# Two branches' gates as seven half-size products: the memory branch's gates and half of the banded one's in a hybrid decoder layer

## The chip, the cores and the metric

The kernel runs on one core of a Trainium2 chip. The metric is device time in microseconds (us) for one execution of the whole layer, from inputs in HBM to the output in HBM; the figure is the median of three runs. A profile of one further execution gives start and length of every instruction. The engines are called as the profile calls them: PE (matrix products; its weight loads are PEld), DVE and ACT (elementwise work), POOL (elementwise work and transfers it issues), SP (issues transfers).

## What is computed

One decoder layer for 512 tokens of width 1024, in float32. Three attention branches work on the normed input `u` (banded attention with sinks, number 0; stick-breaking attention, 1; attention to a memory of 256 entries, 2). Each branch's output goes through a projection of its own and is multiplied by a gate, a sigmoid of a product of `u` with a 1024 x 1024 weight. The sum goes through `w_out`, a norm and a residual, and then a SwiGLU feed-forward part (FFN) of width 2816.

```python
u = rms_norm(h, ln_mix_pre[l])
proj = jnp.einsum('bsd,de->bse', u, w_in[l])
qa, ka, va, qb, kb, vb, qm, gl = jnp.split(proj, split_idx, axis=-1)
...
g = jax.nn.sigmoid(gl.reshape(B, S, N_BRANCH, D))
merged = (g[:, :, 0] * jnp.einsum('bse,ed->bsd', y_swa, w_branch_swa[l])
          + g[:, :, 1] * jnp.einsum('bse,ed->bsd', y_sb, w_branch_sb[l])
          + g[:, :, 2] * jnp.einsum('bse,ed->bsd', y_mem, w_branch_mem[l]))
mix = jnp.einsum('bsd,de->bse', merged, w_out[l])
```

## The kernel before

Every float32 operand of a product is split in two parts, `hi` (rounded, ACT, line 134) and `lo` (the rest, DVE, line 135). A product is three matmuls, hi with hi, lo with hi, hi with lo (`mm3`, lines 166, 168, 169). Activations lie transposed: eight tiles `u[k]` of 128 features x 512 tokens, each as hi and lo (`n0h`, `n0l` to `n7h`, `n7l` in the profile).

The products with weights form one stream, `dn`, a `Stream` of units. A unit is 512 KB of weights (128 x 1024): it is loaded by SP up to four units ahead (`w_load`, three buffers `raw`), split up to three units ahead (`w_split`, four buffers each `hi` and `lo`), and multiplied by a generator of matmuls. Attention is written as generators too; between their steps `dn.run(us)` lets about so many microseconds of the stream through, so that PE has weights to multiply while ACT and DVE work on a softmax. `dn.until(flag)` runs the stream to a mark. A scheduler then orders each engine's instructions by priority, which is the order of writing except where `tc.high_priority()` lifts something, and by what it believes ready.

A gate unit (`proj` with kind `g0`, `g1` or `g2`) gives 128 gate features: 8 slices of K times 3 matmuls of 128 x 512 into one PSUM bank from `dps`, a pool of two banks, then one copy or sigmoid by ACT (lines 301 and 185). Each branch has eight gate units, and then four units of its projection (`branch`, tile `br`), whose results DVE multiplies with the gates (line 444). The order is: stick-breaking gates, four query units `qm`, stick-breaking projection; banded gates `g00` to `g07`, with the banded attention's last step and the scores of the first memory pair (`ms`) around them; banded projection, with the softmax (`mnm`, `mw`) and transposes (`mpt`) of the memory pairs; memory gates `g20` to `g27`; memory projection; `w_out` (`mx`).

The FFN's gate and up products are already made of seven half-size products each (`gu`, tiles `gx`, `gy`, `gw`; 128 x 256 matmuls), in the order p1 p5 p6 p3 p7 p2 p4, with banks from a larger pool, and nine `raw` buffers. There three sums of weights are made by transfers that add into `raw` (POOL queue, line 1015) or by DVE (line 1033); snapshots are copied by ACT (line 1053) and joined by DVE (line 1059).

Of the kernel before, what the change touches and what calls it, by code (L numbers as in the profile page):

```python
# [10 lines left out]
F32 = mybir.dt.float32  # L11
# [6 lines left out]
P = 128  # L18
# [14 lines left out]
class Stream:  # L33
# [12 lines left out]
    def add(self, src, n, mm):  # L46
        self.units.append({"src": src, "n": n, "mm": mm, "load": [], "split": [], "flags": []})
# [56 lines left out]
def tile_kernel(ctx, tc, a):  # L104
# [24 lines left out]

    st = {}  # L130

    def split(raw, hi, lo):

        ins = nc.scalar.copy(hi, raw)  # L134
        lows = nc.vector.tensor_tensor(lo, raw, hi.bitcast(F32), op=ALU.subtract)  # L135
        if "behind" in st:
            after(ins, st["behind"][0])
            after(lows, st["behind"][1])
        return ins
# [2 lines left out]

    def w_load(src, n):
        uid[0] += 1
        raw = wp.tile([P, 1024], F32, tag="raw", name=f"raw{uid[0]}")
        nc.sync.dma_start(raw[:, :n], src)
        return raw

    def w_split(raw, n):
        uid[0] += 1  # L150
        hi = wp.tile([P, 1024], F32R, tag="hi", name=f"hi{uid[0]}", bufs=4)
        lo = wp.tile([P, 1024], F32R, tag="lo", name=f"lo{uid[0]}", bufs=4)
        if isinstance(raw, list):
            for i, x in enumerate(raw):
                ins = split(x[:, :], hi[:, i * 512 : (i + 1) * 512], lo[:, i * 512 : (i + 1) * 512])
        else:
            ins = split(raw[:, :n], hi[:, :n], lo[:, :n])
        if "chain" in st:
            after(ins, st["chain"])
        return hi, lo  # L160
# [22 lines left out]
    def fn(*args, **kw):  # L183

        ins = nc.scalar.activation(*args, **kw)  # L185
        for p in pin:
            after(ins, p)
        since.append(ins)
        return ins
# [140 lines left out]
    def sigmoids(b):  # L330

        st.setdefault("sigmoid", set()).add(b)
        for c in range(8):
            if (f"g{b}", c) in st:
                g = st[(f"g{b}", c)]
                fn(g[:, :], g[:, :], AF.Sigmoid)

    def val(h, q):
        def gen(hi, lo):
# [94 lines left out]
    def branch(b, c2, order):  # L434
        def gen(hi, lo):
            for i in range(2):
                c = 2 * c2 + i
                g = st[(f"g{b}", c)]
                ps = dps(f"br{b}{c}")
                for k in range(4):  # L440
                    mm3(ps[:, :], cols((hi, lo), (i * 4 + k) * P, P), y[(b, k)], k == 0, k == 3)
# [26 lines left out]
    def add_proj(kind, idx, ci):  # L468
        src = a["w_p"][:, ci].rearrange("p k n -> p (k n)")
        dn.add(src, 1024, gate(int(kind[1]), idx) if kind[0] == "g" else proj(kind, idx))  # L470
# [10 lines left out]
    add_proj("qa", 2, 14)  # L481
    add_proj("qa", 3, 15)
    for b, order in ((SB, 0), (SWA, 1), (MEM, 2)):
        for c in range(8):
            add_proj(f"g{b}", c, 17 + 3 * c + b)
        dn.mark(f"gates{b}")
        if b == SB:
            for i in range(4):
                add_proj("qm", i, 8 + i)
        for c2 in range(4):  # L490
            dn.add(a["w_br"][:, b, 2 * c2 : 2 * c2 + 2].rearrange("p c k n -> p (c k n)"), 1024, branch(b, c2, order))
        dn.mark(f"branch{b}")
# [15 lines left out]

    FIRST = 3
    PIECE = ((0, 2), (2, 5), (5, 8))  # L510
    raws = [wp.tile([P, 1024], F32, tag="raw", name=f"raw_first{i}") for i in range(FIRST)]
    his = [wp.tile([P, 1024], F32R, tag="hi", name=f"hi_first{i}", bufs=4) for i in range(FIRST)]
    los = [wp.tile([P, 1024], F32R, tag="lo", name=f"lo_first{i}", bufs=4) for i in range(FIRST)]

# [323 lines left out]
    for c in range(4):  # L838
        for us in swa_pair(c, bias):
            dn.run(us)  # L840
    dn.until(f"gates{SWA}")
    table("sigmoid_and_others")
    sigmoids(SWA)
# [540 lines left out]
def _layout(i):  # L1384
# [10 lines left out]
    heads = np.concatenate([np.r_[c * 64 : c * 64 + 64, 256 + c * 64 : 256 + c * 64 + 64] for c in range(4)])  # L1395
    cols += [heads[c * P : (c + 1) * P] for c in range(4)]
    cols += [np.arange(512, 640)]
    cols += [np.arange(2816 + b * D + c * P, 2816 + b * D + (c + 1) * P) for c in range(8) for b in range(3)]
    w_mem = i["w_mem_kv"][0]
    br = [i["w_branch_swa"][0][heads], i["w_branch_sb"][0], i["w_branch_mem"][0]]  # L1400
    br = np.stack([kpn(w, P) for w in br])
# [46 lines left out]
```

## Time and profile before

| | us |
|---|---|
| median of three runs (811.13 to 811.83) | 811.28 |
| the profiled execution, device time | 811.55 |
| the profiled execution, span of the instructions | 809.4 |

The span and the device time of the same execution differ by 2.15 us, which lie around the instructions. In the profile "busy" is the time in which an engine had an instruction in it; matmuls overlap, so the distance between starts, and not the length of one, tells how fast PE works. The stages by span: projections and stick-breaking attention to 218 us, banded attention with the stick-breaking projection to 281, banded gates to 329, banded projection and memory attention to 365, memory gates to 408, memory projection and `w_out` to 460, then FFN up to about 700 and FFN down to the end.

### The profile page before, as it was taken

Reading aid. Unit: us, or ns where it says so; the run is one execution under the profiler, and the core shown is the slowest. Engines: PE = TensorE matmul, PEld = TensorE weight load, DVE = VectorE, ACT = ScalarE, POOL = GpSimd, SP = SyncE. Lnnn points to the kernel's source line nnn. Section 1 sums busy time; section 2 is a strip of 40 time slices with the busy share of each in tenths; the row PEclk is TensorE's granted clock in tenths of the full one; section 3 lists DMA queues with packets and bytes.
Section 4 is the critical chain, followed back from the end, with each engine's and each line's share of the span. In section 5 each row is a group of like instructions: output and inputs, shape, how many; then the busy total and the mean of one; then the engine's idle time right before and its main releaser. Section 6 shows DMA issues by size and latency. Waiting matters only on the chain.

```text
span 809.4 us, 12343 instructions
## 1 busy us (share of the span) xinstructions
PE 800.0 (99%) x4723; PEld 702.6 (87%) x4723; DVE 575.3 (71%) x917; ACT 458.8 (57%) x824; POOL 84.4 (10%) x103
## 2 busy tenths in 40 slices
PE   9999999999999999999999999999999999999996
PEld 6899788778788888888888899999999999988885
DVE  5898678646378832772284869977676777898797
ACT  6566677666756544552362566654444454666573
POOL 1001210000000000221004100010000000205200
PEclk9999999999999999999999999999999999999999
DMA  8343354211221233213259936987777662759902
GB/s 270 118 143 105 114 186 141 93 53 53 79 79 53 79 88 95 79 53 104 82 162 386 251 56 143 265 217 197 187 181 191 177 170 86 177 132 220 213 0 104
DMA packets 37739, 112.93 MB, mean 140 GB/s; under 512 B 4624, under 2 KB 6176, under 8 KB 37680
## 3 DMA queue, kind: packets, MB, share of 16 engines
q1 hardware_dynamic: 29232, 86.20, 33.5%
q0 software_dynamic: 8016, 25.68, 16.6%
q8 instruction: 37, 0.61, 0.3%
q10 hardware_dynamic: 432, 0.27, 0.1%
q14 instruction: 22, 0.18, 0.1%
HBM read 108.46 MB, written 3.67 MB: 139 GB/s over the span
## 4 chain that ended last, share of the span: by engine, by line
PE 93%; DVE 4%; ACT 2%; issue 1%; DVEq 0%; ACTq 0%
PE g L166 5%; PE g L168 5%; PE g L169 5%; PE gx L169 5%; PE gx L166 5%; PE gx L168 5%; PE z L172 4%; PE br L168 3%; PE br L166 3%; PE br L169 3%; PE x L166 2%; PE x L169 2%; PE x L168 2%; PE gy L169 2%; PE gy L166 2%; PE gy L168 2%
## 5 line engine op out<-in xcount | busy, mean ns | idle before, releaser
L135 DVE TENSOR_TENSOR lo<-raw,hi 128x1024 fp32r<-128x1024 f32 (+2 forms) x64 | 78.8, 1236 | 74.1 <-ACT hi L134 74.1
L134 ACT CAST hi<-gw 128x1024 fp32r<-128x1024 f32 x77 | 79.8, 1047 | 81.4 <-DVE gw L1033 39.8
L134 ACT CAST hi<-raw 128x1024 fp32r<-128x1024 f32 (+2 forms) x64 | 65.7, 1034 | 95.2 <-PE g L168 61.7
L135 DVE TENSOR_TENSOR lo<-gw,hi 128x1024 fp32r<-128x1024 f32 x77 | 93.6, 1224 | 34.0 <-ACT hi L134 33.9
L1015 POOL DMA_DIRECT2D gw<-in_w_gu x27 | 23.4, 896 | 188.2 <-DMA gw<-in_w_gu 81.9
L134 ACT CAST hi<-r 128x1024 fp32r<-128x1024 f32 (+1 forms) x24 | 23.6, 981 | 19.9 <-PE y L169 5.3
L168 PE MATMUL x<-lo,lh 128*128 128x512 f32 x88 | 34.3, 389 | 0.0
L166 PE MATMUL x<-hi,lh 128*128 128x512 f32 x88 | 34.3, 389 | 0.0
L169 PE MATMUL x<-hi,ll 128*128 128x512 f32 x88 | 34.1, 389 | 0.0
L135 DVE TENSOR_TENSOR lo<-r,hi 128x1024 fp32r<-128x1024 f32 (+1 forms) x24 | 27.2, 1135 | 3.7 <-ACT hi L134 3.6
L185 ACT ACTIVATE e<-e 128x384 f32<-128x384 f32 (+1 forms) x48 | 26.9, 561 | 1.5
L679 DVE SCALAR_TENSOR_TENSOR e<-z,e 128x384 f32<-128x384 f32 (+1 forms) x24 | 14.4, 598 | 17.6 <-ACT e L185 17.6
L135 DVE TENSOR_TENSOR lo<-bp,hi 128x512 fp32r<-128x512 f32 x33 | 22.8, 727 | 5.7 <-ACT hi L134 5.6
L134 ACT CAST hi<-bp 128x512 fp32r<-128x512 f32 x33 | 19.2, 620 | 13.3 <-PE y L169 4.8
L169 PE MATMUL gx<-N2h,lo 128*128 128x256 f32 x88 | 25.0, 284 | 0.3 <-DVE lo L135 0.3
L166 PE MATMUL gx<-B11h,hi 128*128 128x256 f32 x88 | 25.1, 285 | 0.2 <-ACT B11h L944 0.2
L166 PE MATMUL mx<-woh,mgh 128*128 128x512 f32 x64 | 25.0, 391 | 0.0
L169 PE MATMUL gw<-B21h,lo 128*128 128x256 f32 x88 | 25.0, 284 | 0.0
L168 PE MATMUL gx<-B11l,hi 128*128 128x256 f32 x88 | 25.0, 284 | 0.0
L169 PE MATMUL mx<-woh,mgl 128*128 128x512 f32 x64 | 24.9, 390 | 0.0
L169 PE MATMUL gy<-T1h,lo 128*128 128x256 f32 x88 | 24.9, 283 | 0.0
L168 PE MATMUL gw<-B21l,hi 128*128 128x256 f32 x88 | 24.9, 283 | 0.0
(764 smaller groups left out, 2797.8 us busy)
## 6 DMA issues: line engine op xcount, KB each, us to landing
gw<-in_w_gu SPq DMA_DIRECT2D x57, 512.0 KB, 5.1
raw<-in_w_p SPq DMA_DIRECT2D x38, 512.0 KB, 3.6
gw<-in_w_gu POOLq DMA_DIRECT2D x27, 512.0 KB, 7.1
raw<-in_w_br SPq DMA_DIRECT2D x12, 512.0 KB, 3.6
bp<-in_w_dn SPq DMA_DIRECT2D x22, 256.0 KB, 8.2
r<-in_w_dn POOLq DMA_DIRECT2D x10, 512.0 KB, 8.3
raw<-in_w_out SPq DMA_DIRECT2D x8, 512.0 KB, 3.6
bp<-in_w_dn POOLq DMA_DIRECT2D x11, 256.0 KB, 12.8
```

What stands on the lines that cost most here:

```text
L134: ins = nc.scalar.copy(hi, raw)
L135: lows = nc.vector.tensor_tensor(lo, raw, hi.bitcast(F32), op=ALU.subtract)
L166: one = nc.tensor.matmul(out, lh, rh, start=start, stop=False, skip_group_check=True)
L168: nc.tensor.matmul(out, *two, start=False, stop=False, skip_group_check=True)
L169: return one, nc.tensor.matmul(out, *three, start=False, stop=stop, skip_group_check=True)
L172: return nc.tensor.matmul(out, l, r, start=start, stop=stop, skip_group_check=True)
L185: ins = nc.scalar.activation(*args, **kw)
L679: nc.vector.scalar_tensor_tensor(x, z[i][:, :n], 0.0, x, op0=ALU.max, op1=ALU.add)
L1015: nc.gpsimd.dma_start(gw[(n, key)][:, :], g_src(n, i, j), accum_op=ALU.add)
```

## The change

For the memory branch, the eight gate units become two groups (`n` = 0, 1) of seven units; of the banded branch, gate units 0, 1, 4, 5 stay, and 2, 3, 6, 7 become one such group (`n` = 1). A group covers four gate tiles: weights are cut in two halves of gate tiles (`f`) by two halves of K (`j`), tokens in two halves of 256. Each unit is still 512 KB of weights, or a sum of such, and 24 matmuls, now of 128 x 256.

- Left sides: p1, p2, p4 use quarters of the weight as loaded. `s` starts as the sum of two quarters (a load, and a POOL transfer that adds) for p5; DVE adds p1's quarter for p6 and then p2's for p3 (`q_sum`), and p3 takes it with the sign turned. `t` is another sum by load and adding transfer, for p7.
- Right sides: p1, p2, p3 use halves of `u` as they are. `rights` builds the sides of p6, p7 and p4 from `u` once (tiles `fx`, `fy`, `ft`, `fp6`, `fp7`, `fp4`, split to `p6r`, `p7r`, `p4r`), after the last banded pair. `right_t1` writes the split of `ft` over the second half of `u[0]` to `u[3]`, for p5, once the last plain gate unit is through.
- Results: bank `x` takes p1, p6, p7 and p4 on top of each other, `y` p5 and p3, `w` p2. ACT copies the bank after p1, p5 and p6 (`qk`); DVE joins after p2, p3 and p7. The three tiles come from the same pool of two banks. Sigmoids are of 128 x 256, eight for a group.
- `raw` has five buffers in place of three. On the host the gate columns of `w_p` stand branch by branch.

```diff
-    def split(raw, hi, lo):
-
-        ins = nc.scalar.copy(hi, raw)
-        lows = nc.vector.tensor_tensor(lo, raw, hi.bitcast(F32), op=ALU.subtract)
+    def split(raw, hi, lo, sign=1.0):
+
+        if sign == 1.0:
+            ins = nc.scalar.copy(hi, raw)
+            lows = nc.vector.tensor_tensor(lo, raw, hi.bitcast(F32), op=ALU.subtract)
+        else:
+            ins = nc.scalar.mul(hi, raw, sign)
+            lows = nc.vector.scalar_tensor_tensor(lo, raw, sign, hi.bitcast(F32), op0=ALU.mult, op1=ALU.subtract)
...
-        raw = wp.tile([P, 1024], F32, tag="raw", name=f"raw{uid[0]}")
+        raw = wp.tile([P, 1024], F32, tag="raw", name=f"raw{uid[0]}", bufs=5)
...
+        for args in st.pop(("raw", b), ()):
+            gate_out(b, *args)
+
+    def gate_out(b, n, i, f, src, sign=1.0):
+
+        for j in range(2):
+            c = 4 * f + 2 * n + j
+            if (b, c) not in quart:
+                quart[(b, c)] = ck(f"g{b}{c}")
+            g = quart[(b, c)]
+            fn(g[:, i * 256 : (i + 1) * 256], src[:, j * 256 : (j + 1) * 256], AF.Sigmoid, scale=sign)
+
+    quart = {}
+    right = {}
+    TILE = dict(p1="x", p6="x", p7="x", p4="x", p5="y", p3="y", p2="w")
+    SEVEN = ("p1", "p2", "p5", "p6", "p3", "p7", "p4")
+    qw, qb_, qk = {}, {}, {}
+
+    def right_of(p, k):
+        if p in ("p1", "p2"):
+            return tuple(x[:, :256] for x in u[k if p == "p1" else 4 + k])
+        if p in ("p5", "p3"):
+            return tuple(x[:, 256:] for x in u[k if p == "p5" else 4 + k])
+        return cols(right[p][k // 2], (k % 2) * 256, 256)
+
+    def q_src(b, n, f, j):
+        c = 17 + 8 * b + 4 * f + 2 * n
+        return a["w_p"][:, c : c + 2, 4 * j : 4 * j + 4].rearrange("p g k n -> p g (k n)")
+
+    def q_raw(b, n, key, f, j):
+        uid[0] += 1
+        raw = wp.tile([P, 1024], F32, tag="raw", name=f"qw{uid[0]}", bufs=5)
+        nc.sync.dma_start(raw[:, :].rearrange("p (g m) -> p g m", g=2), q_src(b, n, f, j))
+        qw[(b, n, key)] = raw
+
+    def q_plus(b, n, key, f, j):
+        raw = qw[(b, n, key)]
+        nc.gpsimd.dma_start(raw[:, :].rearrange("p (g m) -> p g m", g=2), q_src(b, n, f, j), accum_op=ALU.add)
+
+    def q_got(b, n, p):
+        key = {"p5": "s", "p6": "s", "p3": "s", "p7": "t"}.get(p, p)
+
+        def got():
+            if (b, n, key) not in qw:
+                q_raw(b, n, key, *{"p1": (0, 0), "p2": (0, 1), "p4": (1, 1)}[p])
+            raw = qw[(b, n, key)]
+            return (raw, -1.0) if p == "p3" else raw
+
+        return got
+
+    def q_sum(b, n, key):
+        def add():
+            x, y = qw[(b, n, "s")], qw[(b, n, key)]
+            nc.vector.tensor_tensor(x[:, :], x[:, :], y[:, :], op=ALU.add)
+
+        return add
+
+    def q_end(b, n, p, ps):
+        def done(i, f, src, sign=1.0):
+            if b in st.get("sigmoid", ()):
+                gate_out(b, n, i, f, src, sign)
+                return
+            if sign != 1.0:
+                t = ck(f"qr{b}{n}")
+                nc.scalar.mul(t[:, :], src[:, :], sign)
+                src = t
+            st.setdefault(("raw", b), []).append((n, i, f, src))
+
+        def join(t, x, y, op, i, f):
+            nc.vector.tensor_tensor(t[:, :], x[:, :], y[:, :], op=op)
+            done(i, f, t)
+
+        with tc.high_priority():
+            if p in ("p1", "p5", "p6"):
+                qk[p] = ck(f"qk{p}{b}{n}")
+                nc.scalar.copy(qk[p][:, :], ps[:, :])
+            elif p == "p3":
+                t = qk.pop("p6")
+                join(t, t, ps, ALU.subtract, 1, 0)
+            elif p == "p7":
+                t = qk.pop("p5")
+                join(t, t, ps, ALU.subtract, 1, 1)
+            elif p == "p2":
+                t = ck(f"qj{b}{n}")
+                join(t, ps, qk.pop("p1"), ALU.add, 0, 0)
+            else:
+                done(0, 1, ps, -1.0)
+
+    def quarter(b, n, p):
+        def gen(hi, lo):
+            if p in ("p1", "p5", "p2"):
+                qb_[TILE[p]] = dps(f"q{TILE[p]}{b}{n}")
+            ps = qb_[TILE[p]]
+            for j in range(2):
+                for k in range(4):
+                    first = p in ("p1", "p5", "p2") and j == 0 and k == 0
+                    mm3(
+                        ps[:, j * 256 : (j + 1) * 256], cols((hi, lo), (j * 4 + k) * P, P), right_of(p, k), first, k == 3
+                    )
+                    yield 0.36
+            q_end(b, n, p, ps)
+
+        return gen
+
+    def add_quarters(b, n):
+        base = len(dn.units)
+        for p in SEVEN:
+            dn.add(q_got(b, n, p), 1024, quarter(b, n, p))
+            if p in ("p6", "p3"):
+                dn.on_split(q_sum(b, n, "p1" if p == "p6" else "p2"))
+        for key, what, args, back in (
+            ("s", q_raw, (1, 0), 5), ("s", q_plus, (1, 1), 3), ("t", q_raw, (1, 0), 5), ("t", q_plus, (0, 0), 3)
+        ):
+            i = base + SEVEN.index("p5" if key == "s" else "p7") - back
+            dn.units[i]["load"].append(lambda w=what, k=key, x=args: w(b, n, k, *x))
+
+    def rights():
+
+        names = ("p6", "p7", "p4")
+        for c in range(2):
+            for p in names:
+                right.setdefault(p, []).append((ck(f"{p}rh{c}", F32R), ck(f"{p}rl{c}", F32R)))
+            f = {p: ck(f"f{p}{c}") for p in names}
+            for e in range(2):
+                k, sl = 2 * c + e, slice(e * 256, (e + 1) * 256)
+                x, y = ck(f"fx{k}"), ck(f"fy{k}")
+                for t, j in ((x, k), (y, 4 + k)):
+                    nc.vector.tensor_tensor(t[:, :], u[j][0].bitcast(F32), u[j][1].bitcast(F32), op=ALU.add)
+                t1 = ck(f"ft{k}")
+                one = st.setdefault("t1", {})[k] = t1[:, :256]
+                nc.vector.tensor_tensor(one, x[:, 256:], x[:, :256], op=ALU.subtract)
+                n2 = f["p6"][:, sl]
+                nc.vector.tensor_tensor(n2, one, y[:, 256:], op=ALU.subtract)
+                for p, t in (("p7", x), ("p4", y)):
+                    nc.vector.scalar_tensor_tensor(f[p][:, sl], n2, -1.0, t[:, :256], op0=ALU.mult, op1=ALU.subtract)
+                yield
+            for p in names:
+                h, l = right[p][c]
+                split(f[p][:, :], h[:, :], l[:, :])
+            yield
+
+    def right_t1():
+
+        for k, t in st["t1"].items():
+            split(t, u[k][0][:, 256:], u[k][1][:, 256:])
...
-                g = st[(f"g{b}", c)]
+                g = st[(f"g{b}", c)] if (f"g{b}", c) in st else quart[(b, c)]
...
-        for c in range(8):
-            add_proj(f"g{b}", c, 17 + 3 * c + b)
+        if b == MEM:
+            add_quarters(b, 0)
+            add_quarters(b, 1)
+        else:
+            for c in range(8) if b == SB else (0, 1, 4, 5):
+                add_proj(f"g{b}", c, 17 + 8 * b + c)
+        if b == SWA:
+            dn.mark("plain_end")
+            add_quarters(b, 1)
         dn.mark
...
+    for _ in rights():
+        dn.run(2.0)
+    dn.until("plain_end")
+    right_t1()
...
-    cols += [np.arange(2816 + b * D + c * P, 2816 + b * D + (c + 1) * P) for c in range(8) for b in range(3)]
+    cols += [np.arange(2816 + b * D + c * P, 2816 + b * D + (c + 1) * P) for b in range(3) for c in range(8)]
```

**On PE**, between the products that reuse bank `x`, which is read by a join on DVE after p7. Before, in the banded gates, one gate tile (`g04`) is followed at once by the next (`g05`), in the other bank:

```order
L168 MATMUL g04_3006<-n7l_412,hi91_2890 128x512
L169 MATMUL g04_3006<-n7h_411,lo91_2891 128x512
L166 MATMUL g05_3039<-n0h_376,hi93_2936 128x512
L168 MATMUL g05_3039<-n0l_377,hi93_2936 128x512
L169 MATMUL g05_3039<-n0h_376,lo93_2937 128x512
```

After, in the banded group, from the end of p7 (right side `p7r`) to the start of p4 (`p4r`):

```order
L169 MATMUL qx01_3081<-p7rh1_2992,hi99_3142 128x256
L171 MATMUL qx01_3081<-p7rl1_2993,hi99_3142 128x256
L172 MATMUL qx01_3081<-p7rh1_2992,lo99_3143 128x256
L171 MATMUL ms11_3335<-mks0l_1299,qms1h_2326 128x256
L172 MATMUL ms11_3335<-mks0h_1298,qms1l_2327 128x256
L169 MATMUL br00_3388<-y00h_2355,hi104_3209 128x512
L171 MATMUL br00_3388<-y00l_2356,hi104_3209 128x512
L172 MATMUL br00_3388<-y00h_2355,lo104_3210 128x512
L169 MATMUL qx01_3081<-p4rh0_2923,hi101_3175 128x256
L171 MATMUL qx01_3081<-p4rl0_2924,hi101_3175 128x256
```

Two matmuls of a memory pair's scores and three of the banded projection now stand between p7 and p4. In the memory groups eight matmuls of the next group's p1, and four of the memory projection, stand in this place. Between p2 and p5, whose bank `y` is the one that p2's join frees, the first 14, 9 and 14 matmuls of p6 stand in the three groups.

**On DVE**, after the last banded pair. `y03l` is the low part of that pair's output, `lo91` and the like are low parts of weights. Before:

```order
L135 TENSOR_TENSOR lo91_2891<-raw88_2829,hi91_2890 128x1024
L135 TENSOR_TENSOR y03l_2911<-ysw3_2901,y03h_2910 128x512
L135 TENSOR_TENSOR lo93_2937<-raw90_2888,hi93_2936 128x1024
L135 TENSOR_TENSOR lo95_2970<-raw92_2934,hi95_2969 128x1024
L135 TENSOR_TENSOR lo97_3003<-raw94_2967,hi97_3002 128x1024
```

After:

```order
L136 TENSOR_TENSOR lo93_2896<-qw90_2834,hi93_2895 128x1024
L136 TENSOR_TENSOR y03l_2916<-ysw3_2906,y03h_2915 128x512
L467 TENSOR_TENSOR fx0_2928<-n0h_376,n0l_377 128x512
L467 TENSOR_TENSOR fy0_2929<-n4h_396,n4l_397 128x512
L470 TENSOR_TENSOR ft0_2932<-fx0_2928 128x256
L472 TENSOR_TENSOR fp60_2925<-ft0_2932,fy0_2929 128x256
L474 SCALAR_TENSOR_TENSOR fp70_2926<-fp60_2925,fx0_2928 128x256
L474 SCALAR_TENSOR_TENSOR fp40_2927<-fp60_2925,fy0_2929 128x256
L467 TENSOR_TENSOR fx1_2946<-n1h_381,n1l_382 128x512
L467 TENSOR_TENSOR fy1_2947<-n5h_401,n5l_402 128x512
L470 TENSOR_TENSOR ft1_2950<-fx1_2946 128x256
L136 TENSOR_TENSOR lo94_2974<-qw92_2893,hi94_2973 128x1024
```

The building of the right sides stands between the weight splits. From `y03l` to the join after p2 (`qj01`) there are now 41 instructions of some size: 8 sums of 128 x 512, 16 of 128 x 256, 3 weight splits, 6 splits of 128 x 512 and 4 of 128 x 256, 2 weight sums of 128 x 1024, and 2 maxima of the memory scores.

**On ACT**, at the same place. Lines 301 and 304 copy a finished gate tile out of its bank, lines 185 and 188 are the sigmoid. Before:

```order
L134 CAST y03h_2910<-ysw3_2901 128x512
L134 CAST hi93_2936<-raw90_2888 128x1024
L301 ACTIVATE g01_2932<-g01_2894 128x512
L185 ACTIVATE g01_2932<-g01_2932 128x512
L134 CAST hi95_2969<-raw92_2934 128x1024
```

After:

```order
L135 CAST y03h_2915<-ysw3_2906 128x512
L135 CAST hi94_2973<-qw92_2893 128x1024
L135 CAST p6rh0_2919<-fp60_2925 128x512
L135 CAST p7rh0_2921<-fp70_2926 128x512
L135 CAST p4rh0_2923<-fp40_2927 128x512
L304 ACTIVATE g01_2970<-g01_2899 128x512
L135 CAST hi95_3031<-qw82_2622 128x1024
L188 ACTIVATE g01_2970<-g01_2970 128x512
L135 CAST n0h_376<-ft0_2932 128x256
L135 CAST n1h_381<-ft1_2950 128x256
L135 CAST n2h_386<-ft2_3003 128x256
L304 ACTIVATE g04_3029<-g04_2977 128x512
```

The emptying of `g01`'s bank now stands behind three casts that wait for DVE, and that of `g04`'s bank behind three casts that wait for the last plain gate tile `g05` to have read `u`.

## Rows read from the trace of the kernel before

**Rows 1.** The page's head: span, and PE's busy time, share and instructions.
```profile
span 809.4 us, 12343 instructions
PE 800.0 (99%) x4723; PEld 702.6 (87%) x4723; DVE 575.3 (71%) x917; ACT 458.8 (57%) x824; POOL 84.4 (10%) x103
```

**Rows 2.** Every wait of PE in the span: total us, times, longest.
```profile
PE warm L172 <- DVE idle L527: 1.3, 1, 1.3
PE z L172 <- ACT v_all L359: 0.8, 1, 0.8
PE gx L169 <- DVE lo L135: 0.3, 1, 0.3
PE z L172 <- DVE sl L685: 0.2, 1, 0.2
PE gx L166 <- ACT B11h L944: 0.2, 1, 0.2
```

**Rows 3.** Timeline, PE, banded gates: start us, length us; first matmul of three tiles.
```profile
293.65 0.39 PE L166 MATMUL g<-n0h,hi 128*128 128x512 f32 x1
...
299.09 0.39 PE L166 MATMUL g<-n0h,hi 128*128 128x512 f32 x1
...
304.53 0.39 PE L166 MATMUL g<-n0h,hi 128*128 128x512 f32 x1
```

**Rows 4.** Timeline, PE, FFN: first matmul of p7; last of p7, first of p2.
```profile
568.32 0.28 PE L166 MATMUL gx<-T3h,hi 128*128 128x256 f32 x1
...
571.08 0.28 PE L169 MATMUL gx<-T3h,lo 128*128 128x256 f32 x1
571.20 0.28 PE L166 MATMUL gw<-B21h,hi 128*128 128x256 f32 x1
```

**Rows 5.** Timeline, DVE, FFN: sums one behind another; the join after p7.
```profile
557.61 0.42 DVE L1045 SCALAR_TENSOR_TENSOR aq<-gx,sg 128x256 f32<-128x256 f32 x1
557.95 0.68 DVE L1105 TENSOR_TENSOR sq<-aq,aq 128x512 f32<-128x512 f32 x1
558.54 1.22 DVE L1033 TENSOR_TENSOR gw<-gw,gw 128x1024 f32<-128x1024 f32 x1
559.68 0.69 DVE L1105 TENSOR_TENSOR aq<-aq,aq 128x512 f32<-128x512 f32 x1
...
571.40 0.69 DVE L1059 TENSOR_TENSOR gp<-gp,gx 128x512 f32<-128x512 f32 x1 [0.36 <-PE gx L169]
```

**Rows 6.** Timeline, ACT: a half-width activation and a snapshot in FFN.
```profile
556.00 0.41 ACT L185 ACTIVATE sg<-gp 128x256 f32<-128x256 f32 x1
...
563.64 0.58 ACT L1053 COPY gp<-gy 128x512 f32<-128x512 f32 x1
```

**Rows 7.** Timeline, ACT, banded gates: weight split, copy out of the bank.
```profile
293.62 1.05 ACT L134 CAST hi<-raw 128x1024 fp32r<-128x1024 f32 x1 [3.48 <-PE g L168]
294.58 0.59 ACT L301 ACTIVATE g<-g 128x512 f32<-128x512 f32 x1
```

**Rows 8.** Timeline, DVE, banded gates: the last banded pair's low part, a weight split.
```profile
290.17 0.69 DVE L135 TENSOR_TENSOR y03l<-ysw,y03h 128x512 fp32r<-128x512 f32 x1 [1.57 <-ACT y03h L134]
294.70 1.23 DVE L135 TENSOR_TENSOR lo<-raw,hi 128x1024 fp32r<-128x1024 f32 x1 [3.84 <-ACT hi L134]
```

**Rows 9.** Stretches: us, then busy us (count) of PE, PEld, DVE, ACT, POOL; clock, DMA share, GB/s.
```profile
286.00:314.00 28.00, 28.00 (x133) 22.61 (x132) 7.20 (x7) 11.56 (x17) 0.00 (x0) 1.00 0.29 79
...
366.00:408.00 42.00, 42.00 (x187) 34.79 (x186) 9.17 (x8) 12.49 (x17) 0.54 (x1) 1.00 0.33 100
545.00:700.00 155.00, 155.00 (x1286) 154.63 (x1285) 115.91 (x137) 78.79 (x111) 12.03 (x14) 1.00 0.64 168
```

**Rows 10.** Timeline: table load and first exponential (ACT), first scaling (DVE), first transposes (PE).
```profile
328.48 1.28 ACT L193 ACT_TABLE_LOAD   x1
329.92 0.47 ACT L185 ACTIVATE mw<-ms,mnm 128x256 f32<-128x256 f32 x1 [0.16 <-DVE mnm L805]
...
332.10 0.35 DVE L813 TENSOR_SCALAR mw<-mw,mden 128x256 f32<-128x256 f32 x1
...
336.67 1.91 PE L819 MATMUL mpt<-c_ident,mw 128*128 128x128 f32 x16
```

**Rows 11.** The page's DMA issues: queue, count, size, us from issue to landing.
```profile
raw<-in_w_p SPq DMA_DIRECT2D x38, 512.0 KB, 3.6
gw<-in_w_gu POOLq DMA_DIRECT2D x27, 512.0 KB, 7.1
```

More of the change, by code (lines that the diff above doesn't have):

```diff
@@ L152, in w_split @@
         lo = wp.tile([P, 1024], F32R, tag="lo", name=f"lo{uid[0]}", bufs=4)
[L153 to L157, printed above, removed]
+        sign = 1.0
+        if isinstance(raw, tuple):
+            raw, sign = raw
+        ins = split(raw[:, :n], hi[:, :n], lo[:, :n], sign)
         if "chain" in st:
@@ L510, in tile_kernel @@
     PIECE = ((0, 2), (2, 5), (5, 8))
-    raws = [wp.tile([P, 1024], F32, tag="raw", name=f"raw_first{i}") for i in range(FIRST)]
+    raws = [wp.tile([P, 1024], F32, tag="raw", name=f"raw_first{i}", bufs=5) for i in range(FIRST)]
     his = [wp.tile([P, 1024], F32R, tag="hi", name=f"hi_first{i}", bufs=4) for i in range(FIRST)]
```

## The prediction

> **What bounds the kernel now.** I read the page's head first [rows 1]: PE is busy in 800.0 of 809.4 us. Busy is only an upper bound, since matmuls overlap, so the list of PE's waits came next [rows 2]: five in the whole span, 2.8 us together. None lies between the stick-breaking stage's start and FFN, although PE changes there all the time between attention and weights. So PE is the bound, and wherever the change is made, PE's own work is saved one for one unless it turns into a wait. The third view is the distance between equal matmuls. A gate tile of 24 matmuls 128 x 512 takes 299.09 - 293.65 = 5.44 us, and the next one the same [rows 3]: 0.227 us per matmul. An FFN product of 24 matmuls 128 x 256 takes 571.20 - 568.32 = 2.88 us [rows 4]: 0.120 us each, at the same full clock [rows 9]. The half costs 0.53 of the whole.
>
> **What is removed.** A group of four gate tiles costs 4 x 5.44 = 21.76 us. Seven half-size products cost 7 x 2.88 = 20.16 us. That saves 1.60 us for a group, not an eighth (2.72), and 3 x 1.60 = **4.80 us** for the three groups. Everything else that PE does stays.
>
> A rule speaks against the trade. First the rows: half the columns take 0.120 us where the whole takes 0.227 us [rows 3, 4], so the trade pays. The Trainium skill, "TensorE: Matmul & The Clock Gate", section "Back-to-back issue gap", says that in a real stream the spacing is set by weight load and matmul together, and gives about 81 ns for 128 columns and 131 ns for 512. On a straight line that is some 98 ns for 256 columns, an estimate from that page, and a group would go from 12.6 to 16.4 us, three groups 11.6 us slower. The trace of this kernel disagrees with both figures.
>
> **What is added to ACT and DVE in a group.** ACT: seven weight splits of 1.05 [rows 7], three snapshots of 0.58 and eight half sigmoids of 0.41 [rows 6], 12.4 us. DVE: seven splits of 1.23 [rows 8], three joins of 0.69, two weight sums of 1.22 [rows 5], 13.1 us. Both fit into 20.16 us. FFN does the same work and more with DVE busy 116 of 155 us, and PE does not wait there [rows 9]. Cost nothing; the cover is DVE's idle time, about three quarters in the gate stages [rows 9].
>
> **Transfers.** A group moves seven times 512 KB in place of four, 182 GB/s over its 20.16 us, where the gate stages now move 79 to 100 and FFN 168 at a DMA share of 0.64 [rows 9]. A sum by transfer takes a load of 3.6 us and an adding one of 7.1 [rows 11], 10.7 us; both sums are begun five units, 14 us, ahead. The adding transfers stand in POOL's queue before the banded projection's additions, which the memory projection needs only some 60 us later. On SP the banded projection's first weights wait until p1's quarter has been added, about 309 us of the span; they land by 313 and are wanted about 324. Cost nothing, and about 4 us, one load, if a buffer came free late.
>
> **The right sides.** This is the one place with a heavy burden. DVE has 41 instructions between `y03l` at 290.17 [rows 8] and the join after the first p2. By the spacing of instructions that stand close [rows 5], 0.34 for 128 x 256, 0.59 for 128 x 512 and 1.14 for 128 x 1024, they take 20 x 0.34 + 16 x 0.59 + 5 x 1.14 = 21.9 us, so the join starts about 312.7 and ends about 313.4. PE, counted from the rows: `g04` from 293.65, `g05` after two score matmuls to 304.77, p1 to 307.65, fifteen score matmuls to 309.45, p2 to 312.33, 14 matmuls of p6 to 314.0. Then p5 needs the bank that the join frees. So DVE, if it never waits, is 0.6 us early. By full lengths instead of spacings it takes 25.5 us and is 3.1 us late. It also waits for ACT now and then, whose casts wait for `g05`. I take the spacing, because these are sums in a row as in rows 5, and 0.3 us for the waits; bounds 0 and 3.1.
>
> The copies out of banks that now stand behind casts on ACT: `g01`'s is wanted at 299.3, by when ACT has done a split (1.05), three casts of some 0.6 and the copy of 0.59 from 293.6 [rows 7], with the waits for DVE about 298.3. `g04`'s is wanted at 304.8 and comes about 302.5. Nothing, but the margins are 1 and 2 us.
>
> **The joins on banks.** After p7 the last matmul starts at 571.08 and the next slot is 571.20; DVE's join runs 571.40 to 572.09 [rows 4, 5]. So the bank is free 0.89 us after the next slot, 0.93 with a hop back like the one from PE to DVE (0.04). Between p7 and p4 stand 2 x 0.12 + 3 x 0.227 = 0.92 us, 0.96 and 0.91: even. Take 0.1 for the three; the upper bound is a weight split (1.23) that is in the way each time, 3.7. Between p2 and p5 stand 14, 9 and 14 matmuls, 1.68, 1.08 and 1.68 us, more than 0.93. But the join stands on DVE behind the weight split for p6, the sum for p3 and its split. In the second memory group that chain begins when p4 of the first frees a weight buffer: 1.05 + 1.14 + 1.14 + 1.05 + 1.14 with some 0.5 of hops is 6.0, with the join 6.7 us, against 1.92 + 2.88 + 1.68 = 6.48 us of PE. 0.3 us late. In the first memory group the same 6.7 stands against 6.84: nothing.
>
> **The memory softmax.** Now the first scaled weights are ready at 332.45 and PE transposes them at 336.67: 4.2 us to spare [rows 10]. Afterwards ACT has, from p4's end: a weight split 1.05, the turned copy 0.59, eight half sigmoids 3.28, a table load 1.28, four exponentials 1.88, then DVE a reciprocal and a scaling, 0.55: 8.6 us by lengths, some 7.8 by spacings. PE has 34 matmuls in between, 7.7 us. So the margin is gone, and the transposes come 0.1 to 0.9 us late; I take 0.5.
>
> **Five buffers in place of three** bring loads of the first 100 us forward. The waits of 0.8 and 0.2 us [rows 2] there are for ACT and DVE, which are not short of loads at that moment: 0, bounds 0 and a gain of 1.0.
>
> **The sum.** 4.80 saved; 0.3 + 0.1 + 0.3 + 0.5 = 1.2 given back by the single estimates. I take half, 0.6, since the same scheduler has interleaved PE in the same way for 380 us of this trace without a wait [rows 2]. The span goes from 809.4 to 805.2. The profiled execution took 811.55, 0.27 over the median of the three, a difference within their spread. From the median: 811.28 - 4.2 = **807.1 us**.
>
> **Rivals.**
> - *No wait at all, and the start gains.* 811.28 - 4.8 - 0 to 1.0: 805.5 to 806.5, say 805.7. For it: [rows 2]. Against: four places where my own count has no margin.
> - *DVE and ACT come late around the banded group.* With DVE at full lengths p5 waits 3.1 us, and the softmax behind it 0.9: 811.28 - 4.8 + 4.0 = 810.5, with less than all of it 808.4 and up. For it: 41 instructions without a gap where DVE had 7.2 of 28 us [rows 9]. Against: spacings in rows 5.
> - *Slower: the joins are never covered.* If at each of the six hand-overs DVE is busy when PE's last matmul ends, p7 to p4 costs 0.93 + 1.23 - 0.93 = 1.2 us three times, and p2 to p5, behind a sum and a split (2.45), 1.7, 2.3 and 1.7: 9.4 together, so 815.9. It decides for slower from 6.4 us, 1.07 for each hand-over. Against: what stands before the joins can begin a unit or more earlier, as in FFN.
> - *Half-width matmuls are paced by weight loads here.* A load is 0.19 us long by PEld's time over its count, 34.79 for 186 [rows 9]. At that pace a group would take 168 x 0.19 = 31.9 us, and the kernel 811.28 + 3 x 10.2 = 841.8. Against: in FFN loads of 0.120 us, busy in all the time, keep 0.120 [rows 9]. The Trainium skill's section named above is a milder form of this rule.
>
> **How the numbers follow.** Forecast (806.2 to 808.4) 0.64; no wait 0.14; DVE and ACT late 0.13; joins uncovered 0.07; weight loads 0.02. A difference of 0.2%, 1.6 us, is about what a measurement of this kernel can tell from no change: faster is under 809.7, slower over 812.9. Faster: 0.64 + 0.14 + 0.05 of the third = 0.83. Same: 0.08 of the third and 0.02 of the fourth = 0.10. Slower: 0.05 + 0.02 = 0.07. The range from 805.6 to 809.4 leaves out a part of the second, most of the third, the fourth and the fifth: 0.2.
>
> **What would show it.** In the profile after: 2.88 us from one product of a group to the next where nothing stands between, and 504 matmuls of 128 x 256 in place of 288 of 128 x 512; PE's waits, where a p5 that waits for the join, a p4 that waits for the join, and an `mpt` that waits for a scaling are my three places, each under 0.6 us; the first join about 313; `mw` scaled a little after PE has come to it. Wrong would be: a product of more than 2.9 us without a wait in it (weight loads), waits of over 1 us at the joins, or a wait for a load.

## The result and the profile after

The changed kernel takes 813.39 us (median; 811.14 to 813.78) against 811.38 for the kernel before on the same chips: a ratio of 1.0021, interval 1.0011 to 1.0030. Forecast were 807.1 us and a range of 805.6 to 809.4. The profiled execution took 813.66 us with a span of 811.9, 2.5 us more than before, although PE is busy for less.

The page's head, and the five longest waits of PE in the span (us in total, times, longest), answering to [rows 1, 2]; three more, of 0.2 and 0.3 us, are as before:

```profile
span 811.9 us, 12928 instructions
PE 798.1 (98%) x4939; PEld 709.7 (87%) x4939; DVE 619.0 (76%) x975; ACT 476.7 (59%) x861; POOL 91.6 (11%) x109
...
PE mpt L974 <- DVE mw L968: 3.0, 1, 3.0
PE warm L175 <- DVE idle L682: 1.3, 1, 1.3
PE qy L169 <- DVE qj L409: 0.8, 1, 0.8
PE kb L169 <- ACT uh L245: 0.4, 1, 0.4
PE qy L169 <- ACT qkp L415: 0.4, 1, 0.4
```

Three waits are new in the changed stages: for the scaled weights of the memory softmax (`mpt <- mw`), for a join (`qy <- qj`) and for a snapshot (`qy <- qkp`). The list does not show the whole. By windows (stretch, busy us and counts of PE, PEld, DVE, ACT, POOL; clock, DMA share, GB/s) the clock has fallen to its lower level, 1.2 GHz, behind the first of them:

```profile
336.60:339.60 3.00, 0.14 (x1) 0.00 (x0) 3.00 (x1) 0.85 (x4) 2.97 (x3) 1.00 0.62 93
339.60:342.60 3.00, 2.81 (x9) 2.43 (x10) 2.96 (x9) 1.07 (x2) 0.00 (x0) 0.50 0.45 82
```

PE does next to nothing for 3 us, and then works for 3 us at half the clock: matmuls of 128 x 512 start 0.43 us apart (341.13, 341.56, 341.98) in place of 0.227. At half the clock 3 us of work are worth 1.5, so the stretch costs some 1.5 us more than the wait itself.

What held DVE stands in the timelines of DVE, POOL and PE (start, length, instruction; in brackets idle time and its releaser), and before PE's line those of the load that POOL's transfer waited for (SP's issues, and the time to landing of the last):

```profile
332.35 0.69 DVE L592 TENSOR_TENSOR g<-br,g 128x512 f32<-128x512 f32 x1 [2.00 <-PE br L172]
...
334.93 0.62 DVE L968 TENSOR_SCALAR mw<-mw,mden 128x256 f32<-128x256 f32 x2
335.46 0.68 DVE L592 TENSOR_TENSOR g<-br,g 128x512 f32<-128x512 f32 x1
336.06 3.93 DVE L968 TENSOR_SCALAR mw<-mw,mden 128x256 f32<-128x256 f32 x2
...
335.87 1.19 POOL L377 DMA_DIRECT2D qw<-in_w_p  x1 [4.15 <-ACT hi L135]
336.65 2.92 POOL L598 TENSOR_TENSOR g<-g,g 128x512 f32<-128x512 f32 x2
...
320.26 9.88 SPq L372 DMA_DIRECT2D qw<-in_w_p  x4
...
qw<-in_w_p SPq DMA_DIRECT2D x1, 512.0 KB, 5.4
...
339.79 1.12 PE L974 MATMUL mpt<-c_ident,mw 128*128 128x128 f32 x4 [3.05 <-DVE mw L968]
```

Two scalings take 0.62 us, and the next two 3.93, through the whole stretch in which POOL issues an adding transfer and makes two additions. The first of these additions had its operand at 333.04, when DVE's product was done (332.35, 0.69 long). It ran at 336.65, since the adding transfer for the second memory group's `s` stood in front of it in POOL's queue, and that waited until its own load had landed: SP issued it about 329.8, as the last of the four, and it took 5.4 us. (The bracket of POOL's line names ACT, whose split ended at 335.62, later than the load.)

The ledger of the two spans, in us:

| place | rows | difference |
|---|---|---|
| up to the band's bias (`pbias`) | 95.43 for 96.65 | -1.2 |
| products, three groups | 2.88 each, as below | -4.8 |
| hand-overs of banks in the three groups | gaps over 0.12 between starts | +2.5 |
| last product's end to the memory gates | 38.64 and 0.68 of three matmuls moved ahead, for 33.67 | +5.65 |
| the rest, the end included | | +0.3 |

The first and the fourth row are read from these starts on PE: `pbias` before and after, the begin and the end of the fourth row's stretch before, and its begin after (its end after, 366.00, stands further below):

```profile
96.65 0.58 PE L172 MATMUL pbias<-oh,rb 32*128 32x384 f32 x1
95.43 0.91 PE L175 MATMUL pbias<-oh,rb 32*128 32x384 f32 x2
...
329.16 0.40 PE L166 MATMUL br<-y00h,hi 128*128 128x512 f32 x1
362.83 0.39 PE L166 MATMUL g<-n0h,hi 128*128 128x512 f32 x1
...
327.36 0.40 PE L169 MATMUL br<-y01h,hi 128*128 128x512 f32 x1
```

### The profile page after: what moved, and what is told of

Its sections match the earlier page's. It is cut to its first block, busy times and chain, and to the rows that moved or that the text cites. A ratio compares the mean times of both kernels' runs of the same rounds, so it can differ in the third digit from the quotient of the medians.

```text
span 811.9 us, 12928 instructions
## 1 busy us (share of the span) xinstructions
PE 798.1 (98%) x4939; PEld 709.7 (87%) x4939; DVE 619.0 (76%) x975; ACT 476.7 (59%) x861; POOL 91.6 (11%) x109
## 4 chain that ended last, share of the span: by engine, by line
PE 50%; DVE 2%; issue 1%; ACT 1%; DVEq 0%
PE gx L172 5%; PE gx L169 5%; PE gx L171 5%; PE x L172 2%; PE x L171 2%; PE x L169 2%; PE gy L169 2%; PE gy L172 2%; PE gy L171 2%; PE mx L172 2%; PE mx L169 2%; PE mx L171 2%; PE y L172 1%; PE y L171 1%; PE y L169 1%; PE gw L172 1%
## 5 line engine op out<-in xcount | busy, mean ns | idle before, releaser
L135 ACT CAST hi<-raw 128x1024 fp32r<-128x1024 f32 (+2 forms) x52 | 53.1, 1032 | 49.3 <-PE qb L171 11.3
L136 DVE TENSOR_TENSOR lo<-raw,hi 128x1024 fp32r<-128x1024 f32 (+2 forms) x52 | 63.1, 1217 | 18.7 <-ACT hi L135 18.5
L136 DVE TENSOR_TENSOR lo<-qw,hi 128x1024 fp32r<-128x1024 f32 x18 | 22.8, 1264 | 11.2 <-ACT hi L135 11.2
L135 ACT CAST hi<-qw 128x1024 fp32r<-128x1024 f32 x18 | 18.9, 1050 | 16.2 <-issue 6.0
```

## The experiments

**Theory A**: POOL's queue. A transfer that waits at its head lets the additions pile up, and DVE's scaling stands still beside them; PE waits, and its clock falls. **Theory B**: the softmax is late by itself, on ACT, behind a split and eight half sigmoids that the change puts ahead of it. Each time is the median of 5 to 11 executions; the kernel before, run beside them, took 810.96 to 811.16. The changed kernel itself was timed once, beside 811.38, so a difference from its 813.39 is uncertain by the 0.2 to 0.4 us between these.

**e1. One instruction moved in POOL's queue.**

```diff
+        if (b, n, key) == (MEM, 1, "s"):
+            after(ins, st["merge"])
```

(`st["merge"]` is the last of the eight additions, line 598.)

> One instruction moves: the adding transfer for s of the second memory group goes behind the eight additions of the banded projection in POOL's queue (it stood behind the first). Theory A (POOL's queue): that transfer waited at the head of the queue for its load, the additions ran late and back to back, and DVE's scaling of the memory softmax stood still behind them for 3.7 us. Then here the longest scaling is 1.0 to 1.4 us, PE's wait at mpt falls from 3.0 to under 1.5 us, PE's clock does not fall at 340, and the time is 813.4 - 1.6 to 3.1 - 1.6 = 808.7 to 810.2. Theory B (the softmax is late on ACT, behind eight half sigmoids and a split): wait at mpt and time stay, 3.0 us and 813.4.

Measured: 810.37 us, ratio 0.9991 (0.9982 to 1.0000), 3.0 us under the changed kernel and 0.2 over the upper end expected. The instructions of the other four engines stand in the same order as in the changed kernel. POOL and DVE, then the clock in the stretch that was at half before:

```profile
333.17 1.29 POOL L600 TENSOR_TENSOR g<-g,g 128x512 f32<-128x512 f32 x1 [1.40 <-DVE g L594]
336.34 1.27 POOL L600 TENSOR_TENSOR g<-g,g 128x512 f32<-128x512 f32 x1 [1.88 <-DVE g L594]
...
336.11 1.65 DVE L970 TENSOR_SCALAR mw<-mw,mden 128x256 f32<-128x256 f32 x2
339.02 1.14 DVE L970 TENSOR_SCALAR mw<-mw,mden 128x256 f32<-128x256 f32 x4
...
339.60:342.60 3.00, 3.00 (x19) 2.51 (x19) 3.00 (x8) 2.02 (x4) 0.51 (x1) 1.00 0.00 0
```

The additions run as their operands come, one at a time; two scalings take 1.65 in place of 3.93 us; the clock stays. Theory B falls: ACT's work is the same here. A wait of 0.8 us at `mpt` remains, as one addition still meets a scaling.

**e2. The scaling by ACT**, POOL's queue as in the changed kernel.

```diff
-                nc.vector.tensor_scalar(x, x, den[:, n : n + 1], None, op0=ALU.mult)
+                nc.scalar.mul(x, x, den[:, n : n + 1])
```

> The scaling of the memory weights (eight of 128 x 256 for a pair) is done by ACT in place of DVE; POOL's queue is as in the changed kernel. Theory A: POOL's additions no longer hold anything that PE waits for; ACT's scalings end about 337.1 by lengths (exponentials of the first head until 334.7, a weight split, four of 0.41), so PE waits about 1 us at the first transposes and little at the second, and the time is about 813.4 - 3.0 + 1 - 1.6 = 809.8. Theory B: ACT gets eight more operations in front of the transposes, PE waits for 3 us or more, 813.4 to 815.

Measured: 808.84 us, 0.9970 (0.9959 to 0.9982), 1.0 under the expectation, which had PE wait 1 us. There is no wait at `mpt` at all, though ACT has eight more operations for each pair and POOL's pile is longer than in the changed kernel:

```profile
336.28 1.19 POOL L377 DMA_DIRECT2D qw<-in_w_p  x1 [4.41 <-ACT mw L968]
337.06 4.23 POOL L598 TENSOR_TENSOR g<-g,g 128x512 f32<-128x512 f32 x3
```

A pile costs nothing where DVE has no scaling to make beside it. A new wait of 0.9 came at p4 of the first memory group, where DVE made a weight split ahead of the join.

**e3. Only the banded group**, by leaving the memory gates as whole tiles (`for c in range(8) if b != SWA else (0, 1, 4, 5)`).

> Only the banded group is made of seven products; the memory gates are whole tiles again (they read the half of u that t1 has overwritten, so their values are not the gates). No adding transfer stands among the banded projection's additions. Theory A: the wait of 3 us at mpt is gone, although ACT has the same eight half sigmoids ahead of the softmax: 811.4 - 1.2 (five buffers) - 1.6 + 0.3 (joins) + 0.3 to 1.0 (softmax) = 809.2 to 809.9. Theory B: the wait stays and the clock falls: 811.4 - 1.2 - 1.6 + 0.3 + 3.3 + 1.6 = 813.8.

Measured: 810.88 us, 0.9994 (0.9985 to 1.0003); the wait at `mpt` is 0.8, as in e1, and the clock stays. This is theory A again: ACT's eight half sigmoids are there, the adding transfers are not. One addition still meets a scaling (1.65 us for two). The time is 1.0 over the expectation's upper end. That wait was within its term for the softmax and does not explain the miss; the buffers gave 0.7 in place of 1.2 us (e4), PE waits 0.2 for `mpts11l`, and the rest was not traced. The banded group alone is worth nothing: it is 0.4 over e4, so of 1.6 saved some 2.0 are lost in the softmax behind it and in its hand-overs.

**e4. Five raw buffers in the kernel before**, nothing else.

> The kernel before with five buffers for raw weights in place of three, nothing else. The changed kernel is 1.2 us ahead at 95 us of the span, before any gate. If the buffers do that: 811.4 - 1.2 = 810.2. If it comes from another part of the change (the gate columns' order in memory, the scheduler): 811.4.

Measured: 810.43 us, 0.9992 (0.9983 to 1.0001); the profiled span is 808.4, 1.0 under the one of before, and the wait for `v_all` [rows 2] is gone. A wait of 0.9 for `uh` stands in this execution at 6 us, as it does in some runs and not in others (none in e10 and e11); by `pbias` it has cost nothing, since that starts at 95.65, against 96.65 before. So the first 1.2 us of the ledger are the buffers', less what an execution's start varies by. The interval reaches 1, but e10, which holds the same edit, has 0.9980 to 0.9997.

**e5. Bank `y` of the memory groups from the attention's six banks**, which are idle then.

```diff
-                qb_[TILE[p]] = dps(f"q{TILE[p]}{b}{n}")
+                qb_[TILE[p]] = (aps if b == MEM and TILE[p] == "y" else dps)(f"q{TILE[p]}{b}{n}")
```

> The changed kernel, but in the two memory groups the bank y (p5, p3) comes from the attention's six PSUM banks, which stand idle then; POOL's queue and the softmax are as in the changed kernel. If the hand-over of a bank after p2 and the order of p6 that it brings are what costs there, PE's waits of 1.05 and 0.38 us before p5 and of 0.62 before p3 go to under 0.2 each, since all 24 matmuls of p6 then stand between p5 and p3: 813.4 - 1.8 = 811.6, with the wait at mpt and the fall of the clock still there. If DVE and ACT are too slow for a product every 2.88 us, the waits come back at p7, p3 or p4, and the time stays at 813.

Measured: 811.71 us, 1.0011 (1.0002 to 1.0020), 1.7 under the changed kernel, or 1.3 when each is taken against the kernel before beside it; its executions reach from 810.52 to 812.92. Both waits at `qy` are gone, the one at `mpt` is 2.8, and the clock falls to 0.50 behind it. In the changed kernel the two hand-overs look like this (PE, then DVE, POOL and ACT):

```profile
372.72 0.28 PE L172 MATMUL qx<-p6rh,lo 128*128 128x256 f32 x1
373.79 0.39 PE L169 MATMUL qy<-n0h,hi 128*128 128x256 f32 x1 [0.79 <-DVE qj L409]
...
368.58 2.19 DVE L393 TENSOR_TENSOR qw<-qw,qw 128x1024 f32<-128x1024 f32 x1
...
373.05 0.68 DVE L409 TENSOR_TENSOR qj<-qw,qkp 128x512 f32<-128x512 f32 x1
...
367.56 2.13 POOL L598 TENSOR_TENSOR g<-g,g 128x512 f32<-128x512 f32 x1 [2.74 <-DVE g L592]
...
399.06 0.28 PE L172 MATMUL qx<-p6rh,lo 128*128 128x256 f32 x1
399.69 0.39 PE L169 MATMUL qy<-n4h,hi 128*128 128x256 f32 x1 [0.35 <-ACT qkp L415]
...
398.11 1.05 ACT L135 CAST hi<-qw 128x1024 fp32r<-128x1024 f32 x1 [2.40 <-issue]
399.06 0.58 ACT L415 COPY qkp<-qy 128x512 f32<-128x512 f32 x1
```

p5 of the first memory group waits for the join behind a weight sum that took 2.19 us beside POOL's last addition, where a sum alone takes 1.22 [rows 5]. p3 of the second group waits for ACT's snapshot of p5, which stands behind a split. Only ten matmuls of p6, 1.2 us, are left between p5 and p3, since the other fourteen were used up to cover the join before p5. With a bank of its own p5 goes first and all of p6 covers the snapshot.

**e6. The eight additions by DVE in place of POOL.**

```diff
-                    nc.gpsimd.tensor_tensor(acc[:, :], acc[:, :], g[:, :], op=ALU.add)
+                    nc.vector.tensor_tensor(acc[:, :], acc[:, :], g[:, :], op=ALU.add)
```

> The eight additions of the banded projection are made by DVE in place of POOL; POOL keeps the adding transfers in the same order. It tells whether POOL's additions or its adding transfer hold DVE's scaling. Additions: the longest scaling is 0.35 us and the weight sum at 368 takes 1.22 in place of 2.19 us. Transfer: a scaling of up to 1.2 us remains where it meets one. DVE gets 0.68 us more for each of eight additions, of which two stand before the second scaling. PE's wait at mpt 1 to 1.5 us, p5 of the first memory group waits under 0.3, no fall of the clock: 813.4 - 2.0 - 1.4 - 0.8 = 809.2.

Measured: 808.69 us, 0.9971 (0.9960 to 0.9982), 0.5 under the expectation. POOL has the adding transfer alone, at the same moment:

```profile
335.91 1.42 DVE L968 TENSOR_SCALAR mw<-mw,mden 128x256 f32<-128x256 f32 x4
...
335.76 1.19 POOL L377 DMA_DIRECT2D qw<-in_w_p  x1 [7.49 <-DVE mnm L960]
```

Four scalings beside the transfer take 1.42 us, where four alone take 1.14 in e1 (from 339.02). So the additions hold DVE, and the transfer costs it 0.3. It is faster here to add on DVE, which has more to do then, than to leave the sums to POOL in either order.

**e7. Only the memory groups**, all eight banded gates as whole tiles.

> Only the two memory groups are made of seven products; the eight banded gates are whole tiles again. The softmax is not behind half sigmoids then, so it is done before the additions run late: no wait at mpt, no fall of the clock, even with the adding transfer among the additions. 811.2 - 0.7 (five buffers) - 3.2 + 2.5 (hand-overs of the two memory groups as in the changed kernel) = 809.8. If the late additions hit the scaling here too: 813 and more.

Measured: 809.96 us, 0.9986 (0.9977 to 0.9994), 0.2 over the expectation; the waits before p5 and p3 are as in the changed kernel (0.8 and 0.3). No pile forms: the transfer's load lands earlier here, the transfer is issued at 334.59, and one addition (335.37, 1.72 us) stands behind it. That one meets the scalings (2.40 us for four). PE waits 0.5 us at `mpt`, which I had not expected; by the list it waits for ACT's copy of the transposes before (`mpts00h`), not for a scaling. The clock stays.

**e8. e1, e2 and e5 together.**

> Three edits together: scaling by ACT, the adding transfer behind the additions, bank y of the memory groups from the attention's banks. From e2 (808.8): the waits before p5 and p3 of the second memory group (0.38 and 0.62) go; the wait of 1.07 at p4 of the first group, where a weight split stands before the join, may stay. 807.8 if it stays, 806.8 if not.

Measured: 807.05 us, 0.9951 (0.9937 to 0.9965). The waits of PE in the span, and the clock of the whole:

```profile
PE warm L175 <- DVE idle L684: 1.3, 1, 1.3
PE kb L169 <- ACT uh L245: 0.6, 1, 0.6
PE gx L172 <- DVE lo L136: 0.3, 1, 0.3
PE z L175 <- DVE sl L842: 0.2, 1, 0.2
PE gx L169 <- ACT B11h L1105: 0.2, 1, 0.2
...
core 0: 805.3 us, clock 0.999
```

No wait that the list shows is left in the changed stages. The time lies between the two expected.

**e9. A filler for PE's idle time.** It failed as an experiment.

> The changed kernel with 32 small matmuls of a constant (bf16, 128 x 128, overwritten afterwards) between the first and the second pair of transposes, in the stretch in which PE has nothing to do. The wait for DVE's scaling is not shortened, only filled. If PE's idle time is what lets the clock fall, the clock stays at 1.00 after 340, the six matmuls of 128 x 512 there take 1.4 in place of 2.6 us, and the time is 813.4 - 1.3 = 812.1 with the wait itself still paid (the second transposes at about 339.7). If the clock falls for another reason, the time stays at 813.4 or rises.

Measured: 816.52 us, 1.0057 (1.0043 to 1.0070). The scheduler put the banded projection's nine matmuls, which stood between the transposes, behind them, so PE ran dry twice:

```profile
335.97 1.95 PE L175 MATMUL mpt<-idle 128*128 128x128 bf16 x32
339.74 0.70 PE L977 MATMUL mpt<-c_ident,mw 128*128 128x128 f32 x4 [1.82 <-DVE mw L968]
341.71 1.94 PE L977 MATMUL mpt<-c_ident,mw 128*128 128x128 f32 x8 [1.26 <-DVE mw L968]
```

The clock fell all the same, so nothing follows on what a busy PE would have kept. That the fall goes with the idle time rests on e1 to e3 and e6 to e8, which have no such wait and no fall, and on e5, which keeps both. It is argued from these; no run changes the idle time alone.

**e10. A control**: the kernel before, with e4's buffers and e2's scaling.

> A control for e8: the kernel before, whole gate tiles, with five raw buffers and with the scaling of the memory weights by ACT. There the scaling has 4.2 us to spare, so nothing is expected of it: 810.4 as with five buffers alone. If the scaling by ACT were a gain of its own, it would be under 810.

Measured: 810.23 us, 0.9989 (0.9980 to 0.9997), as with the buffers alone. The scaling by ACT is no gain of its own.

**e11. e5 and e6 together.**

> e5 and e6 together: bank y of the memory groups from the attention's banks, and the banded projection's additions by DVE. From e6 (808.7) the waits before p5 and p3 go (0.63, 0.27, 0.51 and 0.1 for each restart, 1.8 in all): 806.9; the wait of 0.39 at p4 may grow to 1.1, then 807.6.

Measured: 806.78 us, 0.9946 (0.9933 to 0.9958), the lowest of all, though its interval overlaps e8's; 4.3 us under the kernel before beside it and 3.5 under e10. No wait of PE in the list lies between 90 and 469 us.

## Why the prediction was wrong

The sign was wrong and the time 6.3 us off. Step by step:

- **The saving** was right to the hundredth. A product takes 2.88 us in the new groups too:

```profile
366.00 0.28 PE L169 MATMUL qx<-n0h,hi 128*128 128x256 f32 x1
368.88 0.28 PE L169 MATMUL qw<-n4h,hi 128*128 128x256 f32 x1
```

  Once nothing else is in the way (e8, e11), the time is 3.9 and 4.3 us under the kernel before, with 0.7 to 0.9 of it the buffers' (e4, e10). The rival of weight loads is refuted. But not all of the 4.80 arrives: from the end of the banded attention to the first `mx` PE takes 139.06 us in e10 (288.10 to 427.16) and 135.39 in e11 (288.05 to 423.44), so 3.7 are saved. The other 1.1 lie in no listed wait: between these points some starts on PE come 0.1 to 0.2 us late, at four hand-overs of banks and around the transposes of the memory attention. The prediction had 0.1 for a part of these and no term for the rest.
- **The step that failed is "Transfers"**, in its sentence on POOL's queue. It put the adding transfers "before the banded projection's additions, which the memory projection needs only some 60 us later", and cost that at nothing. The additions' results were indeed not needed. But I looked only at who reads what POOL makes, not at who stands still while POOL makes it. Late additions run back to back, and beside them two scalings of 0.62 us took 3.93. The wait of 3.05 us that this made at `mpt`, and the clock, are most of the 5.65 us. The prediction had named that wait as one of its three places, at under 0.6. The price was in the trace of before, in rows that I did not read:

```profile
332.97 1.91 DVE L813 TENSOR_SCALAR mw<-mw,mden 128x256 f32<-128x256 f32 x3
...
333.14 1.32 POOL L450 TENSOR_TENSOR g<-g,g 128x512 f32<-128x512 f32 x1 [61.55 <-DVE g L444]
...
335.00 1.14 DVE L813 TENSOR_SCALAR mw<-mw,mden 128x256 f32<-128x256 f32 x4
```

  Three scalings took 1.91 us beside one addition, and four alone 1.14 (three alone 0.88, at 341.25 in the changed kernel). One addition holds DVE by 1.0; the pile held it by about its sum, 3.3 us for a transfer and two additions. It cost nothing there because of the 4.2 us to spare [rows 10], and the same prediction said that the change uses these up.

  The Trainium skill, "SBUF — State Buffer", section "Who interferes with whom", has the rule: VectorE and GpSimd share one pair of SBUF ports, and whichever issues first holds it for its whole instruction while the other is blocked. By the same section of the Trainium skill, `tensor_scalar` on DVE can take that pair, in a mode that uses two ports, and an operation with two inputs in SBUF contends with a GpSimd instruction that reads SBUF. The scalings (two in 3.93 us beside two additions, in 0.62 alone) and the weight sum (2.19 beside one addition, 1.22 alone) agree with it.
- **The right sides**: I took 0.3 us. The join ends at 312.74 and p5 starts without a wait at 313.05: nothing lost. DVE kept the spacing of sums in a row, as taken.
- **p7 to p4**: 0.1 for the three; measured 0.1 in each, 0.3. The fillers were enough, as counted.
- **p2 to p5**: 0.3 in the second memory group, measured 0.37. In the first, nothing, measured 1.04: the sum of 6.7 us against 6.84 was right but for the weight sum's 2.19 us beside POOL. It is the same omission, an addition beside DVE, though this addition ran on time (367.56, operand at 367.42).
- **p6 to p3** was not in the prediction: 0.20 in the banded and 0.61 in the second memory group. I counted what covers the join before p5, and not that the same matmuls are then missing behind it.
- **The softmax**: "0.1 to 0.9 late" holds without the pile. In e6 and e2, where nothing holds the scaling, the transposes wait for under 0.2 us.
- **Five buffers**: 0, with a gain of 1.0 as the bound; measured 0.7 to 1.2. The wait for `v_all` went with them, so it hung on the buffers after all; on which load was not followed.
- **Half of the single estimates** was taken because the scheduler had interleaved without a wait for 380 us. The changed stage is the one in which that margin was spent, so the past stretch was no evidence.
- **The rivals**: the slower one had the wrong mechanism. Its price, 9.4 us, is near what was lost (8.2), but from uncovered joins only 2.5 came.

## What to carry to other kernels

A queue that a new instruction is put into has to be read twice: for what waits for its results, and for what its later work will then run beside. POOL's work is not free where DVE has scalings of a tile or sums of two SBUF tiles on the critical path; moved to DVE it can cost less than it held up (e6). A wait of some 3 us on PE should be priced with the slow stretch that may follow it; and matmuls that cover one hand-over are no longer there to cover the next.

## What the runs showed of the hardware

- After 3 us with almost no matmul PE's granted clock was 0.50 for about 3 us of full work (windows above), some 1.5 us. It does not follow every execution alike: in the ten of the changed kernel the mean clock is 0.995 or 0.996 in eight, and 0.998 and 0.997 in the two shortest (811.14 and 811.97 us). Only one of the ten was profiled, so whether the wait was shorter in those two is not known. The edited kernels without that wait spread over 0.2 to 0.6 us, this kernel's executions over 2.6; but those of the kernel before, which has no such wait either, spread over 1.2 to 2.0, so the spread alone shows nothing of the clock.
- It goes both ways. POOL's additions take 1.27 to 1.3 us alone; in the kernel before, one that came 0.16 us behind the start of a weight split on DVE (336.66, 1.22 long) took 2.20 (336.82), and the split kept its length. The addition of 2.13 at 367.56 began beside such a split too, and DVE's weight sum behind it then took 2.19. Behind an adding transfer the first addition is listed 0.4 us before the transfer's issue has ended, and the additions are longer by about as much: 1.72 for one (e7), 2.92 for two, 4.23 for three (e2).
- An adding transfer's issue (1.19 us on POOL) cost four scalings beside it 0.3 us; an addition of 1.3 us cost them 1.0.
- The first matmul after a wait for a bank starts the second 0.22 in place of 0.12 us later (373.79 to 374.01), so that each of these waits costs 0.1 more than the list of waits says.
